# Stick-breaking attention taken from right to left, its scans cut in two pieces

## The chip, the cores and the metric

The kernel runs on one core of one Trainium2 chip. The metric is the device time of one execution in microseconds (us). TensorE is called PE, VectorE DVE, ScalarE ACT and GpSimd POOL, as in the profile.

## The reference

Two layers of a decoder trunk on 1024 tokens of width 1024: RMSNorm, two token mixers side by side (a dilated sliding-window attention and a stick-breaking attention) behind gates, a residual, then a gated ConvFFN and a residual. The change touches only the stick-breaking attention, four heads of 64 in each layer:

```python
def block(args):                       # 128 queries of block i, all heads
    z = jnp.einsum('bhqc,bhkc->bhqk', q_blk, kt) * scale
    causal = key_pos[None, :] < qpos[:, None]
    log_stay = jnp.where(causal, jax.nn.log_sigmoid(-z), 0.0)
    later = lax.cumsum(log_stay, axis=3, reverse=True) - log_stay
    attn = jnp.where(causal, jnp.exp(jax.nn.log_sigmoid(z) + later), 0.0)
    return jnp.einsum('bhqk,bhkc->bhqc', attn, vt)
```

Each weight is sigmoid(z) of its own key times the product of (1 - sigmoid(z)) over all later keys up to the query. The kernel forms that product of the later keys directly, as a running product from the right end of a row to its left end.

## The kernel before

Nearly all matmuls run in fp32 pieces: an operand is split into a high and a low part (ACT casts, DVE subtracts; `split`, lines 129 and 130), and products are sums of several matmuls.

PE's instructions are issued in the order in which the program writes them. In the mixers the order on DVE, ACT and POOL is chosen when the kernel is built, by priorities and a cost model; `tc.high_priority` moves an instruction ahead.

The stick-breaking work of a layer is 16 **items**, made by `stick_item(pr, s, qp)`: four heads (pr, s), and for each head qp = 0 to 3. An item covers two query blocks of 128 (its rows a = 0 and 1; block i = 2qp + a), and row a has L = 128 (i + 1) keys. An item has two score steps and qp + 1 pairs of a turn and an apply:

- `score(a)` (lines 610 to 628) computes the scores of one row in chunks of up to 512 keys from left to right into a PSUM bank (tag `s`, two banks; PE, lines 584 and 585). DVE adds the mask to the last 128 columns (line 623). ACT writes `beta` = sigmoid(z) (line 624) and `stay` = sigmoid(-z) (line 625). DVE then scans the whole row of `stay` from right to left (line 627) and multiplies `beta` by it, shifted by one (line 628).
- `turn(kb)` transposes the 128 x 128 blocks of the key blocks kb and kb + 1, of both rows, on PE (line 638) and splits them (`sbh`, `sbl`). `apply(kb)` multiplies them with the values (line 649) into one PSUM bank over all kb. The turns go from kb = 0 to kb = 2qp; the last one holds the diagonal blocks, and after its apply `fold` adds the two halves.

Both rows' `beta` tiles have the tag `p4` (four buffers, two for each item). `stay` holds both rows of an item and has the tag `e8` (six buffers, shared with the keys, queries and the output of this attention).

`attend` runs the items one after the other and weaves in the score steps of the next: with the sequence turn, late apply of the item before, turn, apply, ... of an item of qp + 1 turns, the first score step of the next item stands ahead of the first entry and the second one some way into the sequence. Behind every entry `dense.advance(rate)` issues pieces of other projections (`k_ps`, `q_ps`, `v_ps`, `r_ps`), 0.68 of a step for each entry in this stage, so that PE has work between the parts of an item. The neighbouring attention stages and the FFN are not touched.

Of the kernel before, what the change touches and what calls it, by code (L numbers as in the profile page):

```python
# [6 lines left out]
F32 = mybir.dt.float32  # L7
# [3 lines left out]
AF = mybir.ActivationFunctionType  # L11
ALU = mybir.AluOpType
# [3 lines left out]
P = 128  # L16
T = 1024
# [27 lines left out]
AHEAD = 200  # L45
# [7 lines left out]
def trunk_kernel(ctx, tc, x, norm1, w_in, b_gate, w_br, w_o, norm2, w_up, conv_w, conv_b, w_down, norm_f, out, depth=None, probe=None):  # L53
    nc = tc.nc
    act, dve, pe, pool = nc.scalar, nc.vector, nc.tensor, nc.gpsimd
# [4 lines left out]
    sb = ctx.enter_context(tc.tile_pool(name="sb", bufs=1))  # L60
# [10 lines left out]
    zero = cp.tile([P, 1], F32, name="zero")  # L71
    pool.memset(zero, 0.0)
    mask_b = cp.tile([P, P], BF16, name="mask_b")
# [42 lines left out]
    def bank(tag, name):  # L116
        return ps.tile([P, 512], F32, tag=tag, name=name)
# [4 lines left out]
    def big(name, dtype=F32):  # L122
        return sb.tile([P, 2, T], dtype, tag="e8", bufs=6, name=name)
# [459 lines left out]
    def scores(o, qt, ql, k):  # L583
        pe.matmul(o, qt, k, start=True, stop=False, skip_group_check=True)
        pe.matmul(o, ql, k, start=False, stop=True, skip_group_check=True)

    def parts(src, n, name):

        hi, lo = small(name + "h", F32R), small(name + "l", F32R)
        with tc.high_priority(offset=AHEAD):  # L590
            split(hi[:, :n], lo[:, :n], src[:, :n])
        return hi, lo

    def fold(dst, o):

        n = o.shape[-1]
        tmp = small("fold")
        with tc.high_priority(offset=AHEAD):
            act.copy(tmp[0:64, :n], o[64:128, :])
            dve.tensor_tensor(dst, o[0:64, :], tmp[0:64, :n], ALU.add)  # L600


    def stick_item(pr, s, qp):
        if "ob" not in R:
            R["ob"] = big("ob")
        q, k, vt, ob = R["qb", pr], R["kb", pr], R["vb"], R["ob"]
        hd = 2 * pr + s
        rows, st, shared = {}, {}, {}

        def score(a):  # L610
            i = 2 * qp + a
            L = P * (i + 1)
            bt = rows[a] = sb.tile([P, T], F32, tag="p4", bufs=4, name="beta")
            if a == 0:
                st[0] = big("stay")
            sv = st[0][:, a, :]
            for c0 in range(0, L, 512):
                w = min(512, L - c0)
                z = bank("s", "z")
                scores(z[:, :w], *(t[:, s, i * P : i * P + P] for t in q), k[:, s, c0 : c0 + w])  # L620
                with tc.high_priority(offset=AHEAD):
                    if c0 + w == L:
                        dve.tensor_tensor(z[:, w - P : w], z[:, w - P : w], mask_b, ALU.add)
                    act.activation(bt[:, c0 : c0 + w], z[:, :w], AF.Sigmoid)
                    act.activation(sv[:, c0 : c0 + w], z[:, :w], AF.Sigmoid, scale=-1.0)  # L625
            rev = sv[:, 0:L][:, ::-1]
            dve.tensor_tensor_scan(rev, rev, zero[:, 0:1].to_broadcast([P, L]), 1.0, ALU.mult, ALU.add)  # L627
            dve.tensor_tensor(bt[:, 0 : L - 1], bt[:, 0 : L - 1], sv[:, 1:L], ALU.mult)

        def blocks(kb):  # L630

            return [(j, a) for j in range(2) for a in range(2) if kb + j <= 2 * qp + a]

        def turn(kb):
            tp = bank("t", "sb_t")
            todo = blocks(kb)
            for c, (j, a) in enumerate(todo):
                pe.transpose(tp[:, c * P : c * P + P], rows[a][:, (kb + j) * P : (kb + j + 1) * P], ident)
            shared[kb] = parts(tp, len(todo) * P, "sb")

        def apply(kb):
            last = kb == 2 * qp
            if kb == 0:
                shared["o"] = bank("o", "sb_o")[:, :256]
            o = shared["o"]
            for j in range(2):
                c = P if last and j else 0
                for p in (0, 1):
                    pe.matmul(
                        o[:, c:256],  # L650
                        vt[(kb + j) // 4][:, (kb + j) % 4, hd, :],
                        shared[kb][p][:, 256 * j : 256 * j + 256 - c],
                        start=(kb == 0 and j == 0 and p == 0),
                        stop=(last and j == 1 and p == 1),
                        skip_group_check=True,
                    )
            if last:
                fold(ob[64 * s : 64 * s + 64, pr, qp * 256 : (qp + 1) * 256], o)
                if (pr, s, qp) == (1, 1, 3):
                    nc.sync.dma_start(obd, ob)  # L660

        sc = [lambda: score(0), lambda: score(1)]
        return sc, [(lambda kb=kb: turn(kb), lambda kb=kb: apply(kb)) for kb in range(0, 2 * qp + 2, 2)]


    def near_item(pr, s):
# [479 lines left out]
    def mixer(l, pending):  # L1146
# [37 lines left out]
        for pr in range(2):  # L1184
            for i in range(8):
                needs = ["b1"] if pr else []
                items.append((f"B{pr}{i}", needs, [], RATE[0], lambda pr=pr, i=i: stick_item(pr, i // 4, i % 4)))
# [687 lines left out]
```

## Time and profile before

| what | value |
|---|---|
| median of 3 runs | 2715.49 us (2715.37 to 2717.81) |
| the profiled execution | 2714.47 us, its span 2712.6 us |
| mean granted clock of PE | 0.997 |
| busy share of PE / DVE / ACT / POOL | 98% / 78% / 49% / 27% |
| stick-breaking items, layer 1 | about 69 to 231 us of the span |
| stick-breaking items, layer 2 | about 1410 to 1576 us of the span |

A row of the timeline gives start, duration, engine, line, operation, output and inputs, partitions x elements, and in square brackets the idle time of the engine ahead of it with what ended that. PEld is PE's weight load. A row of the waits gives who waited for whom, the sum in us, how many times, and the longest. Matmuls are pipelined, so a matmul of 512 columns shows 0.39 us but the next one can start 0.23 us after it.

### The profile page before, as it was taken

What the parts mean: (1) busy time and instruction counts of PE and PEld (TensorE: products, weight loads), DVE (VectorE), ACT (ScalarE), POOL (GpSimd) and SP (SyncE); (2) the same over time, 40 slices, a digit from 0 to 9 for tenths busy, and PEclk for the clock granted to TensorE, in tenths of its full rate; (3) what the DMA queues carried; (4) which work ended last, traced back from release to release, by engine and by line L of the source; (5) the groups of instructions that cost most, each with busy time, mean ns of one, the idle gap of its engine ahead of it and who ended that gap; (6) DMA issues with size and microseconds to landing.
All of it is one profiled execution on the core that took longest, in us unless ns stands there. A gap on an engine that the chain in (4) does not pass through costs nothing. (4 is left out here: it accounts for less than half of the span.)

```text
span 2712.6 us, 37003 instructions
## 1 busy us (share of the span) xinstructions
PE 2657.8 (98%) x13098; PEld 2227.5 (82%) x13098; DVE 2105.9 (78%) x3104; ACT 1330.4 (49%) x2458; POOL 742.1 (27%) x537
## 2 busy tenths in 40 slices
PE   8999999999999999999999989999999999999999
PEld 8877788888888888888888778888788888888888
DVE  6877876675789988897658888766858888998865
ACT  5656534464455555432335665434545545554225
POOL 2004133322233434321220041332212433443210
PEclk9999999999999999999999999999999999999999
DMA  4023389863235444688401234997722444446863
GB/s 153 20 80 123 123 229 246 207 226 121 85 117 171 141 154 147 223 320 320 154 32 36 84 111 136 250 230 211 248 85 79 148 152 143 171 141 253 333 246 122
DMA packets 397637, 445.72 MB, mean 164 GB/s; under 512 B 21660, under 2 KB 318988, under 8 KB 395916
## 3 DMA queue, kind: packets, MB, share of 16 engines
q1 hardware_dynamic: 397452, 443.35, 51.4%
q8 instruction: 104, 1.70, 0.3%
q14 instruction: 81, 0.66, 0.1%
HBM read 300.61 MB, written 142.67 MB: 163 GB/s over the span
## 5 line engine op out<-in xcount | busy, mean ns | idle before, releaser
L130 DVE TENSOR_TENSOR w_lo<-up_a,w_hi 128x512 fp32r<-128x512 f32 x240 | 237.2, 995 | 20.5 <-ACT w_hi L129 20.5
L129 ACT CAST w_hi<-up_a 128x512 fp32r<-128x512 f32 x240 | 149.5, 623 | 184.1 <-PE u_a L890 45.6
L1631 DVE TENSOR_TENSOR x<-x,d_ps 128x512 f32<-128x512 f32 (+1 forms) x228 | 152.2, 672 | 76.9 <-PE d_ps L1625 76.0
L1362 POOL TENSOR_TENSOR cv<-cv 128x512 f32<-128x512 f32 x88 | 132.1, 1513 | 248.8 <-DVE cv L1357 138.9
L130 DVE TENSOR_TENSOR w_lo<-w_raw,w_hi 128x512 fp32r<-128x512 f32 x176 | 132.5, 756 | 67.8 <-ACT w_hi L129 67.3
L129 ACT CAST w_hi<-w_raw 128x512 fp32r<-128x512 f32 x176 | 109.2, 621 | 125.9 <-PE o_ps L156 68.6
L129 ACT CAST w_hi<-in_a 128x512 fp32r<-128x512 f32 x140 | 86.8, 620 | 147.6 <-PE i_a L890 83.2
L130 DVE TENSOR_TENSOR g<-cv,g 128x512 fp32r<-128x512 f32 x154 | 152.4, 991 | 5.2 <-ACT g L129 2.7
L1623 PE MATMUL d_ps<-gd_in,w_hi 128*128 128x512 f32 (+1 forms) x340 | 130.2, 383 | 1.3 <-ACT w_hi L129 1.1
L1625 PE MATMUL d_ps<-gd_in,w_lo 128*128 128x512 f32 (+1 forms) x340 | 129.8, 382 | 0.0
L1624 PE MATMUL d_ps<-gd_in,w_hi 128*128 128x512 f32 (+1 forms) x340 | 129.7, 382 | 0.0
L889 PE MATMUL u_a<-hh,w_hi 128*128 128x512 f32 x320 | 124.7, 390 | 0.5 <-DVE u L1513 0.5
L889 PE MATMUL u_a<-t_hi,w_hi 128*128 128x512 f32 x320 | 124.6, 389 | 0.0
L891 PE MATMUL u_a<-t_hi,w_lo 128*128 128x512 f32 x320 | 124.5, 389 | 0.0
L890 PE MATMUL u_a<-hl,w_hi 128*128 128x512 f32 x320 | 124.5, 389 | 0.0
L891 PE MATMUL u_a<-hh,w_lo 128*128 128x512 f32 x320 | 124.5, 389 | 0.0
L890 PE MATMUL u_a<-t_lo,w_hi 128*128 128x512 f32 x320 | 124.5, 389 | 0.0
L130 DVE TENSOR_TENSOR w_lo<-in_a,w_hi 128x512 fp32r<-128x512 f32 x140 | 116.0, 828 | 4.1 <-ACT w_hi L129 3.7
L1018 POOL TENSOR_TENSOR in_a<-in_a 128x512 f32<-128x512 f32 x28 | 38.0, 1357 | 278.9 <-DVE w_lo L130 278.9
L627 DVE TENSOR_TENSOR_SCAN stay<-stay,zero 128x128 f32<-128x128 f32 (+3 forms) x64 | 89.0, 1390 | 32.2 <-ACT stay L625 31.6
L1623 PE MATMUL d_ps<-gd_in,wd 128*128 128x512 f32 (+1 forms) x292 | 113.9, 390 | 0.0
L129 ACT CAST g<-cv 128x512 fp32r<-128x512 f32 x154 | 95.0, 617 | 38.2 <-POOL cv L1362 29.7
(390 smaller groups left out, 8747.7 us busy)
## 6 DMA issues: line engine op xcount, KB each, us to landing
gd<-g SPq DMA_DIRECT2D x154, 512.0 KB, 3.7
gd_in<-gd SPq DMA_DIRECT2D x154, 512.0 KB, 6.4
up_a<-in_w_up_dram SPq DMA_DIRECT2D x80, 512.0 KB, 5.8
in_a<-in_w_in_dram SPq DMA_DIRECT2D x56, 512.0 KB, 6.2
w_raw<-in_w_in_dram SPq DMA_DIRECT2D x104, 256.0 KB, 3.0
t_kq<-tk SPq DMA_DIRECT2D x64, 384.0 KB, 7.8
wd_raw<-in_w_down_dram SPq DMA_DIRECT2D x22, 1024.0 KB, 13.0
gin<-gs SPq DMA_DIRECT2D x32, 512.0 KB, 4.4
```

What stands on the lines that cost most here:

```text
L129: act.copy(hi, src)
L130: dve.tensor_tensor(lo, src, f32(hi), ALU.subtract)
L627: dve.tensor_tensor_scan(rev, rev, zero[:, 0:1].to_broadcast([P, L]), 1.0, ALU.mult, ALU.add)
L889: pe.matmul(o, w[0][:, c], rh, start=(first and i == 0), stop=False, skip_group_check=True)
L890: pe.matmul(o, w[0][:, c], rl, start=False, stop=False, skip_group_check=True)
L891: pe.matmul(o, w[1][:, c], rh, start=False, stop=(last and i == 3), skip_group_check=True)
L1018: pool.tensor_tensor(a11, a22, a11, ALU.subtract)
L1362: return lambda: pool.tensor_tensor(dst, a, b, ALU.subtract)
L1623: pe.matmul(o[:, sub], wh[:, c], gh[:, sub], start=(i == 0 and k in (0, 4, 5)), stop=False, skip_group_check=True)
L1624: pe.matmul(o[:, sub], wh[:, c], gl[:, sub], start=False, stop=False, skip_group_check=True)
L1625: pe.matmul(o[:, sub], wl[:, c], gh[:, sub], start=False, stop=(i == m - 1), skip_group_check=True)
L1631: dve.tensor_tensor(x, x, o[:, sub], ALU.add)
```

## The change

Items with qp of 2 and 3 (five to eight key blocks in a row) are scored from right to left. The first score step now does the right parts (keys from 512 on) of both rows, the second one the left parts (keys 0 to 511) of both rows; the scan of a left part starts from the last value of the right one, and each part has a product of its own. Items with qp of 0 and 1, whose rows have at most 512 keys, keep one step for each row. In all items ACT writes `stay` ahead of `beta`, both `beta` tiles are taken at the first step, and turns and applies go from the diagonal (kb = 2qp) down to kb = 0.

```diff
-        def score(a):
+        def begin():
+            for a in range(2):
+                rows[a] = sb.tile([P, T], F32, tag="p4", bufs=4, name="beta")
+            st[0] = big("stay")
+
+        def score(a, c0):
             i = 2 * qp + a
             L = P * (i + 1)
-            bt = rows[a] = sb.tile([P, T], F32, tag="p4", bufs=4, name="beta")
-            if a == 0:
-                st[0] = big("stay")
-            sv = st[0][:, a, :]
-            for c0 in range(0, L, 512):
-                w = min(512, L - c0)
-                z = bank("s", "z")
-                scores(z[:, :w], *(t[:, s, i * P : i * P + P] for t in q), k[:, s, c0 : c0 + w])
-                with tc.high_priority(offset=AHEAD):
-                    if c0 + w == L:
-                        dve.tensor_tensor(z[:, w - P : w], z[:, w - P : w], mask_b, ALU.add)
-                    act.activation(bt[:, c0 : c0 + w], z[:, :w], AF.Sigmoid)
-                    act.activation(sv[:, c0 : c0 + w], z[:, :w], AF.Sigmoid, scale=-1.0)
-            rev = sv[:, 0:L][:, ::-1]
-            dve.tensor_tensor_scan(rev, rev, zero[:, 0:1].to_broadcast([P, L]), 1.0, ALU.mult, ALU.add)
-            dve.tensor_tensor(bt[:, 0 : L - 1], bt[:, 0 : L - 1], sv[:, 1:L], ALU.mult)
+            bt, sv, w = rows[a], st[0][:, a, :], min(512, L - c0)
+            z = bank("s", "z")
+            scores(z[:, :w], *(t[:, s, i * P : i * P + P] for t in q), k[:, s, c0 : c0 + w])
+            with tc.high_priority(offset=AHEAD):
+                if c0 + w == L:
+                    dve.tensor_tensor(z[:, w - P : w], z[:, w - P : w], mask_b, ALU.add)
+                act.activation(sv[:, c0 : c0 + w], z[:, :w], AF.Sigmoid, scale=-1.0)
+                act.activation(bt[:, c0 : c0 + w], z[:, :w], AF.Sigmoid)
+            rev = sv[:, c0 : c0 + w][:, ::-1]
+            right = 1.0 if c0 + w == L else sv[:, c0 + w : c0 + w + 1]
+            dve.tensor_tensor_scan(rev, rev, zero[:, 0:1].to_broadcast([P, w]), right, ALU.mult, ALU.add)
+            e = min(c0 + w, L - 1)
+            dve.tensor_tensor(bt[:, c0:e], bt[:, c0:e], sv[:, c0 + 1 : e + 1], ALU.mult)
...
         def apply(kb):
-            last = kb == 2 * qp
-            if kb == 0:
+            first = kb == 2 * qp
+            if first:
                 shared["o"] = bank("o", "sb_o")[:, :256]
...
-            if last:
+            if kb == 0:
                 fold(ob[64 * s : 64 * s + 64, pr, qp * 256 : (qp + 1) * 256], o)
...
-        sc = [lambda: score(0), lambda: score(1)]
-        return sc, [(lambda kb=kb: turn(kb), lambda kb=kb: apply(kb)) for kb in range(0, 2 * qp + 2, 2)]
+        def part(a):
+            if a == 0:
+                begin()
+            if qp < 2:
+                score(a, 0)
+            else:
+                for b in range(2):
+                    score(b, 0 if a else 512)
+
+        return [lambda: part(0), lambda: part(1)], [(lambda kb=kb: turn(kb), lambda kb=kb: apply(kb)) for kb in range(2 * qp, -2, -2)]
```

More of the change, by code (lines that the diff above doesn't have):

```diff
@@ L646, in apply @@
             for j in range(2):
-                c = P if last and j else 0
+                c = P if first and j else 0
                 for p in (0, 1):
@@ L652, in apply @@
                         shared[kb][p][:, 256 * j : 256 * j + 256 - c],
-                        start=(kb == 0 and j == 0 and p == 0),
-                        stop=(last and j == 1 and p == 1),
+                        start=(first and j == 0 and p == 0),
+                        stop=(kb == 0 and j == 1 and p == 1),
                         skip_group_check=True,
                     )
-            if last:
+            if kb == 0:
                 fold(ob[64 * s : 64 * s + 64, pr, qp * 256 : (qp + 1) * 256], o)
```

## The prediction

> **What bounds the kernel now.** I read the page first, then the stretches of the two layers in which the stick-breaking items run (69 to 231 us and 1410 to 1576 us), then the waits of TensorE in them.
>
> ```profile
> PE 2657.8 (98%) x13098; PEld 2227.5 (82%) x13098; DVE 2105.9 (78%) x3104; ACT 1330.4 (49%) x2458; POOL 742.1 (27%) x537
> 69.00:231.00 162.00, 153.20 (x900) 131.45 (x899) 132.97 (x202) 100.05 (x211) 3.79 (x4) 0.99 0.21 62
> 1410.00:1576.00 166.00, 155.42 (x902) 133.08 (x901) 135.38 (x201) 98.81 (x210) 9.12 (x9) 0.98 0.20 60
> ```
>
> TensorE (PE) is busy 98% of the span, so time is to be had only where PE stands still. The stretch rows give length, then busy time of PE, weight loads, VectorE (DVE), ScalarE (ACT) and GpSimd, then the granted clock: PE idles 8.8 + 10.6 = 19.4 us in the two stretches, DVE works 82% of them, and the DMA share is 0.2. The waits of PE there, layer by layer (us, times, longest):
>
> ```profile
> PE sb_t L638 <- DVE beta L628: 7.5, 6, 2.2
> PE sb_t L638 <- DVE beta L628: 9.2, 8, 2.2
> PEld z L584 <- ACT stay L625: 2.0, 4, 0.9
> PEld z L584 <- ACT stay L625: 1.9, 3, 0.9
> ```
>
> So 16.7 of the 19.4 us are transposes (L638) that wait for the product of L628. Which items are they? An item is one head and two query blocks; I call items 0 to 3 by qp. Four waits belong to items 0 and 1:
>
> ```profile
> 78.93 0.55 PE L638 MATMUL sb_t<-ident,beta 128*128 128x128 f32 x3 [0.94 <-DVE beta L628]
> 1414.26 0.33 PE L638 MATMUL sb_t<-ident,beta 128*128 128x128 f32 x1 [0.24 <-DVE beta L628]
> 1416.48 0.66 PE L638 MATMUL sb_t<-ident,beta 128*128 128x128 f32 x2 [1.89 <-DVE beta L628]
> 1423.36 0.55 PE L638 MATMUL sb_t<-ident,beta 128*128 128x128 f32 x3 [0.51 <-DVE beta L628]
> ```
>
> They make 3.6 us. The other ten, 13.1 us, are first turns of items 2 and 3 of the later heads: each time the first of four transposes (query row 0) runs and the second (row 1) stands. The longest, with its chain:
>
> ```profile
> 175.47 0.40 PE L584 MATMUL z<-kt,qt 128*128 128x512 f32 x1
> 175.93 0.40 PE L584 MATMUL z<-kt,qt 128*128 128x512 f32 x1
> 179.10 0.30 DVE L623 TENSOR_TENSOR z<-z,mask_b 128x128 f32<-128x128 f32 x1
> 180.56 2.29 DVE L627 TENSOR_TENSOR_SCAN stay<-stay,zero 128x1024 f32<-128x1024 f32 x1 [1.15 <-ACT stay L625]
> 183.21 1.22 DVE L628 TENSOR_TENSOR beta<-beta,stay 128x1023 f32<-128x1023 f32 x1
> 182.01 0.30 PE L638 MATMUL sb_t<-ident,beta 128*128 128x128 f32 x1
> 184.48 0.90 PE L638 MATMUL sb_t<-ident,beta 128*128 128x128 f32 x3 [2.17 <-DVE beta L628]
> ```
>
> Row 1's scores are done at 176.4 (a pair of 512 takes 0.46, 175.47 to 175.93), DVE gets to the mask at 179.1, the whole row must be scanned (2.29) and multiplied (1.22), and only then may its leftmost block be transposed, 2.4 us after PE came for it.
>
> **First turns from the right part.** After the change the first turn of items 2 and 3 takes blocks 2qp and 2qp+1, which lie in columns 512 and up. For both rows these are scored, scanned and multiplied in the first step. That step is issued where row 0 is now: for item 3, before the whole seq of item 2's turns, some 13 us before the first turn (row 0's scores now start at 168.56, quoted below; first turn 182.01). The waits of these ten go. The idle figure understates each: from 182.01 to 184.48 are 2.47 us where 0.06 would do, so 2.41 lost for 2.17 shown, 0.24 more. Ten times: 13.1 + 2.4 = 15.5 us. The bounds are 13.1 (idle alone) and 17 (add the two first-head items 3, which show only in the weight loads, 0.5 us each, and a little more of the overlap). I take 15.5 + 0.5 = 16.0.
>
> **The clock after the long waits.** Six matmuls before and after the wait at 184.48:
>
> ```profile
> 180.45 0.40 PE L155 MATMUL r_ps<-hh,w_hi 128*128 128x512 f32 x1
> 181.84 0.22 PE L584 MATMUL z<-kt,qt 128*128 128x128 f32 x1
> 185.04 0.78 PE L155 MATMUL r_ps<-hh,w_hi 128*128 128x512 f32 x1
> 187.72 0.28 PE L649 MATMUL sb_o<-sbh,vb 128*128 128x256 f32 x1
> 184.00:186.00 2.00, 1.52 (x5) 1.37 (x6) 1.99 (x5) 0.73 (x3) 0.00 (x0) 0.56 0.00 0
> 1528.00:1532.00 4.00, 3.11 (x10) 2.54 (x11) 3.94 (x7) 1.24 (x5) 0.00 (x0) 0.64 0.22 65
> 230.00:234.00 4.00, 4.00 (x24) 3.49 (x25) 2.97 (x9) 3.00 (x5) 0.00 (x0) 1.00 0.59 172
> ```
>
> Six take 1.39 us from 180.45 and 2.68 us from 185.04; the granted clock there is 0.56. That is 1.2 us lost behind the wait (less 0.1 that any turn costs), and the twin in layer 2 (0.64 over four us) as much: 2.4 us come back with the waits. Behind item 3 of the last head (230 to 234 us) the clock stays at 1.00, so I count two only. The Trainium skill, "TensorE: Matmul & The Clock Gate", section "What's actually happening", has the clock halved after at least one idle window of about 3.4 us; this trace disagrees, since it fell behind an idle of 2.17 us. By that rule these waits would be too short to cost any clock, nothing would come back here, and the sum below would be smaller by these 2.4 us.
>
> **ACT writes stay ahead of beta.** A scan needs only stay. In item 1 (one chunk of 512, nothing else changed) DVE stands at the scan until ACT has done both sigmoids:
>
> ```profile
> 160.08 1.23 DVE L627 TENSOR_TENSOR_SCAN stay<-stay,zero 128x512 f32<-128x512 f32 x1 [0.70 <-ACT stay L625]
> 162.08 0.31 PEld L638 LDWEIGHTS sb_t<-ident,beta 128*128 128x128 f32 x3 [0.36 <-DVE beta L628]
> 1551.37 0.31 PEld L638 LDWEIGHTS sb_t<-ident,beta 128*128 128x128 f32 x3 [0.42 <-DVE beta L628]
> ```
>
> A sigmoid of 512 is about 0.5 us of ACT, less than the 0.70 of idle, so scan and product come 0.5 us sooner. The small waits of item 1, four of this kind (first and last shown), go: 1.2 us of their 1.5. The four waits of the first heads quoted above hang on a loaded DVE; I leave them.
>
> **What it costs.** DVE gets a second scan and a second product for each row of items 2 and 3: 2 items, 4 heads, 2 layers, 2 rows, 32 of each.
>
> ```profile
> L627 DVE TENSOR_TENSOR_SCAN stay<-stay,zero 128x1024 f32<-128x1024 f32 x8 | 18.3, 2292 | 9.2 <-ACT stay L625 9.2
> L627 DVE TENSOR_TENSOR_SCAN stay<-stay,zero 128x512 f32<-128x512 f32 x8 | 9.8, 1225 | 5.5 <-ACT stay L625 5.4
> L628 DVE TENSOR_TENSOR beta<-beta,stay 128x1023 f32<-128x1023 f32 x8 | 9.7, 1216 | 0.1
> L628 DVE TENSOR_TENSOR beta<-beta,stay 128x511 f32<-128x511 f32 x8 | 5.5, 682 | 0.1
> ```
>
> 2 x 1.225 - 2.292 = 0.16 and 2 x 0.682 - 1.216 = 0.15 us, so 32 x 0.31 = 9.9 us of DVE, against some 60 us in which DVE idles in the two stretches: no charge on PE. No row shows a scan whose start value is a column; I bound it by 0 and by one more fixed part (0.16 x 32 = 5 us of DVE, also covered) and take 0; a gain I exclude, as nothing is left out. Matmuls, sigmoids, masks and transposes keep their number and widths; no DMA is moved, SP and POOL get nothing, and the store of ob stays behind the last apply.
>
> The scores of item 2's first step become 128 and 256 wide, where they were 512 and 128. The second of them waits today for the bank that item 1's last sigmoid frees (the z rows above). That bank comes free at the same time, but PE arrives earlier: a 512 pair takes 0.46 us, a 128 pair 0.17 (181.84 to 182.01). Six items 2 wait already: 6 x 0.29 = 1.7 us, at most 8 x 0.29 = 2.3.
>
> The second turn of an item now needs the left part, two scans and two products of 512. In item 2 it is close:
>
> ```profile
> 164.31 0.39 PE L584 MATMUL z<-kt,qt 128*128 128x512 f32 x1
> 168.56 0.39 PE L584 MATMUL z<-kt,qt 128*128 128x512 f32 x1
> 170.40 0.95 DVE L628 TENSOR_TENSOR beta<-beta,stay 128x767 f32<-128x767 f32 x1
> 173.64 0.60 PE L638 MATMUL sb_t<-ident,beta 128*128 128x128 f32 x4
> ```
>
> Today DVE ends the item at 171.35. With the same work in another order and 4 x 0.15 more it ends at about 172.0; the second turn, its 0.6 us of wait ahead gone, comes at 173.0. So 1 us in hand, which not every item will have; I take 0.2 us for each of 8, 1.6 us (between 0 and 3). In item 3 the second turn needs only the right part and the left one has several us.
>
> **Sum:** -16.0 - 2.4 - 1.2 + 1.7 + 1.6 = -16.3 us. The profiled execution took 2714.47 us (span 2712.6), the median is 2715.49: 2698.2 by the first, 2699.2 by the second, which I give. Bounds of the same case: -13.1 - 1.0 + 2.3 + 3 = -8.8 (no clock back) gives 2707; -17 for the waits, -2.9 for the clock (twice 0.36 of 4 us), -1.5 for item 1 and -1.9 for the first-head wait at 1416.48, with no new cost, is -23.3 and gives 2692.
>
> **Rivals.** *The wait moves to the second turn* of items 2 and, by less, 3. For it: DVE takes 2.7 us to reach a mask (176.4 to 179.1), and a margin of 1 us is less. Against: in the same stretch its total work grows by 0.6 us only. If 2.5 us get in front, each of 8 waits 1.5 us: 12 of the 16 are given back, about 2711.
>
> *Slower: the one stay buffer holds ACT, and ACT holds the score banks.*
>
> ```profile
> 216.38 0.60 ACT L625 ACTIVATE stay<-z 128x512 f32<-128x512 f32 x1 [1.40 <-DVE beta L628]
> ```
>
> The new item's first write of stay stands until the old item's last product. With stay ahead of beta this wait is at the head of the step; behind it on ACT queue the other three sigmoids, and the casts of the turns. Four sigmoids of item 3's right parts take some 1.8 us, then both z banks come free for the second step, whose scores PE issues 6 us after the first step's. It decides once left products end after 173.1 (174.9, that is 175.47 less the 0.6 us saved, minus 1.8), 1.1 us later than I put them. At 3 us late, 8 items 3 wait 1.9 us for a bank and 8 items 2 wait 2 us at the second turn: 31 us added, 16 saved, about 2730. Against: today's stall of 1.4 us does not reach PE.
>
> *The change doesn't do what it says:* if order is kept by whole tiles, the first turn waits for the left products as well, the waits stay and grow by the 0.3 to 0.6 us that DVE has more in each of 16 items, some 7 us: about 2722. Against it, these:
>
> ```profile
> 68.91 0.68 DVE L537 SCALAR_TENSOR_TENSOR ql<-q_ps,qt 64x512 fp32r<-64x512 f32 x1 [1.07 <-ACT qt L536]
> 69.50 0.28 PE L585 MATMUL z<-kt,ql 128*128 128x128 f32 x1
> 69.61 0.69 DVE L538 SCALAR_TENSOR_TENSOR ql<-q_ps,qt 64x512 fp32r<-64x512 f32 x1
> ```
>
> The matmul at 69.50 reads other columns of ql while two writes that stand before it in the program are still unfinished: order is kept by region.
>
> **How the numbers follow.** Forecast 0.75, wait at the second turn 0.10, held banks 0.10, whole tiles 0.05. About 0.2% (5.4 us) can be told from no change. Below 2710.1 lies the forecast: faster 0.75. Between falls most of the second case and a little of the others: same 0.11. Slower 0.14. The range runs from the forecast's best, 2692, to 2713, which takes in the second case.
>
> **What would show it.** Right: the group PE sb_t waiting for beta falls from 16.7 to about 4 us, no granted clock below 0.9 behind item 3 of the third heads, scans x96 with sum near 94 us, z waits near 6 us. Wrong: a new wait of the second turn on L628's product, waits of z on stay's sigmoid above 10 us, or first turns that still wait for a 512-wide left product.

## The result and the profile after

The kernel after takes 2702.5 us (median of 4 runs, 2699.0 to 2704.0); the kernel before, run beside it, 2716.4 us (4 runs, 2715.4 to 2717.8). The ratio is 0.995, with a 95% interval of 0.9938 to 0.9963. The forecast was 2699.2 us in a range of 2692 to 2713. The profiled execution after took 2702.83 us (span 2700.9), 11.6 us less than the one of before.

Two stretches of the timeline that hold the stick-breaking items of layers 1 and 2 up to the last item's first turns (length, then busy time and count on PE, weight loads, DVE, ACT and POOL, granted clock, DMA share, GB/s):

```profile
69.00:225.00 156.00, 150.61 (x904) 131.62 (x903) 136.42 (x234) 98.16 (x211) 3.80 (x4) 1.00 0.21 63
1403.00:1563.00 160.00, 152.03 (x909) 132.51 (x908) 138.74 (x233) 97.45 (x210) 9.81 (x9) 1.00 0.21 62
```

PE idles 5.4 + 8.0 = 13.4 us where it idled 19.4, and DVE's share grows from 82% to 87%: 6.8 us more work in shorter stretches. The stretches used so far, before and after, stop 12 to 14 us before the last turn of a layer, which starts at 243.7 and 1588.5 us before (not at 231 and 1576, as the table of the profile before has it) and at 236.6 and 1576.9 after. From the first score product to the end of that turn PE idles 21.1 us before and 15.9 after. The waits of PE in the same two stretches (who waited for whom, us in sum, times, longest):

```profile
PE r_ps L155 <- DVE ql L538: 1.9, 1, 1.9
PE z L584 <- ACT beta L625: 1.4, 3, 0.6
PE sb_t L640 <- DVE beta L630: 1.3, 1, 1.3
PE sb_o L651 <- DVE sbl L130: 0.7, 2, 0.4
...
PE sb_t L640 <- DVE beta L630: 3.2, 2, 1.9
PE z L584 <- ACT beta L625: 2.1, 3, 1.2
PE r_ps L155 <- DVE ql L538: 1.9, 1, 1.9
PE sb_o L651 <- DVE sbl L130: 0.8, 2, 0.4
```

Over the whole run the transposes wait 4.5 us for the beta product instead of 16.6, and all three waits that are left are of first heads: the ten of items 2 and 3 are gone. In their place stands a wait that the page of before does not have: a product `r_ps` of the gate projection waits for the second half of an eviction of queries (line 538). The place that answers to the chain shown of before, item 3 of the third head in layer 1, on DVE and PE:

```profile
173.34 0.69 DVE L630 TENSOR_TENSOR beta<-beta,stay 128x511 f32<-128x511 f32 x1
...
177.50 2.46 DVE L628 TENSOR_TENSOR_SCAN stay<-stay,zero 128x512 f32<-128x512 f32 x2
179.87 1.27 DVE L630 TENSOR_TENSOR beta<-beta,stay 128x512 f32<-128x512 f32 x2
...
183.72 0.69 DVE L538 SCALAR_TENSOR_TENSOR ql<-q_ps,qt 64x512 fp32r<-64x512 f32 x1
```

```profile
180.25 0.51 PE L640 MATMUL sb_t<-ident,beta 128*128 128x128 f32 x3
184.57 0.47 PE L155 MATMUL r_ps<-hh,w_hi 128*128 128x512 f32 x1 [1.95 <-DVE ql L538]
```

The right parts of both rows are multiplied by 174.0, six us before the first turn comes for them at 180.25. The left ones end at 181.1, less than a us after that turn, while row 1's product before ended at 184.4. So even the left parts are some 3 us earlier, although DVE has more to do. PE then stands until 184.4 for a query eviction that DVE reaches last. Before, the same eviction ended two us later, and no wait for it shows there; PE was late itself (the third head's first turn and the slow clock behind it):

```profile
185.83 0.70 DVE L538 SCALAR_TENSOR_TENSOR ql<-q_ps,qt 64x512 fp32r<-64x512 f32 x1
```

Two more long waits of after, out of PE's timeline, and then the granted clock (the figure behind the POOL count) in four stretches: the two places where it had fallen before, 184 and 1528 us, and behind these two waits:

```profile
1409.35 0.44 PE L640 MATMUL sb_t<-ident,beta 128*128 128x128 f32 x2 [1.94 <-DVE beta L630]
1568.74 0.39 PE L584 MATMUL z<-kt,qt 128*128 128x256 f32 x1 [1.96 <-DVE st L702]
```

```profile
184.00:188.00 4.00, 3.43 (x18) 2.96 (x19) 3.01 (x8) 1.74 (x5) 0.00 (x0) 1.00 0.58 187
1410.00:1414.00 4.00, 2.75 (x15) 2.21 (x14) 3.78 (x8) 2.91 (x7) 0.00 (x0) 1.00 0.03 8
1528.00:1532.00 4.00, 4.00 (x25) 3.42 (x24) 2.08 (x3) 2.01 (x4) 0.00 (x0) 1.00 0.85 245
1568.00:1572.00 4.00, 3.26 (x10) 2.75 (x11) 3.08 (x11) 3.15 (x9) 0.00 (x0) 0.63 0.40 128
```

In this execution it stays at 1.00 until 1568 us, while the last item's turns still run, and falls there. How much of that is the kernel and how much chance, two more stretches show, the first of before, behind the wait of 1.89 us at 1416.48 that the prediction quotes without its clock, the second of the kernel after, profiled again:

```profile
1416.00:1420.00 4.00, 3.52 (x10) 2.88 (x11) 3.00 (x7) 2.55 (x6) 0.00 (x0) 0.57 0.00 0
186.00:190.00 4.00, 4.00 (x14) 3.28 (x14) 1.59 (x5) 0.59 (x1) 0.00 (x0) 0.57 0.42 138
```

So before has a third fall, and in the second profile of the kernel after the clock falls behind the very wait that left it at 1.00 in the first (`r_ps` for `ql`, 1.95 us in both). Each fall in these traces lasts 3.4 us at half clock, or twice that, so one of 3.4 us costs PE at most 1.7 us. The scans and products of DVE, all shapes together (sum, mean ns; then the idle time of DVE ahead of them and what ended it), after and then before:

```profile
L628 DVE TENSOR_TENSOR_SCAN stay<-stay,zero 128x128 f32<-128x128 f32 (+2 forms) x96 | 93.2, 981 | 10.1 <-ACT stay L624 9.4
L630 DVE TENSOR_TENSOR beta<-beta,stay 128x127 f32<-128x127 f32 (+2 forms) x96 | 54.1, 570 | 6.2 <-ACT sbh L129 0.5
```

```profile
L627 DVE TENSOR_TENSOR_SCAN stay<-stay,zero 128x128 f32<-128x128 f32 (+3 forms) x64 | 89.0, 1390 | 32.2 <-ACT stay L625 31.6
L628 DVE TENSOR_TENSOR beta<-beta,stay 128x127 f32<-128x127 f32 (+3 forms) x64 | 49.0, 766 | 0.9
```

DVE works 9.3 us more in them, and stands 22 us less at a scan for its sigmoid. This second number is the one that I had not looked at, although two of the rows that the prediction quotes carry 9.2 and 5.4 us of it.

### The profile page after: what moved, and what is told of

Its sections match the earlier page's. It is cut to its first block, busy times and chain, and to the rows that moved or that the text cites. A ratio compares the mean times of both kernels' runs of the same rounds, so it can differ in the third digit from the quotient of the medians.

```text
span 2700.9 us, 37123 instructions
## 1 busy us (share of the span) xinstructions
PE 2651.9 (98%) x13098; PEld 2228.1 (82%) x13098; DVE 2106.5 (78%) x3168; ACT 1327.4 (49%) x2458; POOL 746.4 (28%) x537
## 5 line engine op out<-in xcount | busy, mean ns | idle before, releaser
L1633 PE MATMUL d_ps<-gd_in,wd 128*128 128x512 f32 (+1 forms) x292 | 113.9, 390 | 0.0
L418 POOL TENSOR_TENSOR nrm<-nrm,sq 128x512 f32<-128x512 f32 x29 | 40.6, 1399 | 264.2 <-ACT sq L416 263.5
L1635 PE MATMUL d_ps<-gd_in,wd 128*128 128x512 f32 (+1 forms) x292 | 112.8, 386 | 0.0
```

The costliest lines, as they stand in the source:

```text
L418: (adds or (dve if e % 3 == 1 else pool)).tensor_tensor(acc, acc, sq, ALU.add)
L1633: pe.matmul(o[:, sub], wh[:, c], gh[:, sub], start=(i == 0 and k in (0, 4, 5)), stop=False, skip_group_check=True)
L1635: pe.matmul(o[:, sub], wl[:, c], gh[:, sub], start=False, stop=(i == m - 1), skip_group_check=True)
```

## The experiments

I compare two things: the time against the kernel before on the same chip, and the length of the stages, from the first score product of a layer's items to their last turn, both layers summed. That length comes from one profiled execution. The kernel after, profiled twice, gave 167.3 + 173.3 = 340.5 and 169.6 + 171.2 = 340.8 us: a single layer can differ by 2.3 us between executions, so I read nothing into sums that lie within 2 or 3 us of each other. The column on the half clock is what PE lost by it in these stages at most (the time at half clock, halved). All 20 falls of the 14 profiled executions (the 13 of the table and the first of after) stand behind waits of PE of 1.80 to 2.84 us; 19 other waits of that size left the clock at 1.00, one of 2.65 us among them. Which waits of this size cost clock is chance as far as these runs show, so two stage lengths are best compared with this column taken off.

| kernel | median us | ratio to before, 95% interval | stages us | of it by half clock, us | DVE idle at the scan for `stay`: us, times | turns waiting for beta: us, times |
|---|---|---|---|---|---|---|
| before | 2717.9, 2717.4, 2717.4 | 1 | 352.5 | 5.1 | 31.6, 39 | 16.6, 14 |
| turns_only | 2716.1 | 0.9996 (0.9987 to 1.0004) | 350.4 | 3.4 | 29.7, 39 | 16.0, 16 |
| act_order | 2706.8 | 0.9957 (0.9946 to 0.9969) | 344.4 | 1.7 | 19.3, 36 | 9.0, 9 |
| order_and_turns | 2705.6 | 0.9959 (0.9947 to 0.997) | 342.5 | 0 | 19.3, 36 | 8.8, 9 |
| pieces_only | 2707.5 | 0.9963 (0.995 to 0.9975) | 342.4 | 1.7 | 16.4, 21 | 9.8, 14 |
| beta_first | 2705.2 | 0.9956 (0.9943 to 0.9969) | 344.8 | 5.1 | 16.5, 21 | 5.2, 8 |
| left_first | 2706.7 | 0.9955 (0.9942 to 0.9968) | 341.9 | 1.7 | 9.3, 18 | 6.4, 9 |
| row_by_row | 2712.9 | 0.9989 (0.9979 to 0.9998) | 347.4 | 5.1 | 12.7, 24 | 2.8, 2 |
| queries_ahead | 2711.2 | 0.998 (0.9971 to 0.9989) | 342.8 | 5.1 | 11.5, 22 | 3.2, 2 |
| after_again | 2703.2 | 0.9947 (0.9935 to 0.996) | 340.8 | 1.7 | 9.4, 18 | 4.5, 3 |
| mask_pe | 2696.7 | 0.9923 (0.991 to 0.9935) | 333.6 | 0 | 15.5, 13 | 2.6, 3 |
| start_more | 2715.3 | 0.999 (0.9981 to 0.9999) | 354.2 | 5.1 | 13.6, 26 | 2.8, 2 |
| dve_load | 2716.6 | 0.9997 (0.9988 to 1.0006) | 340.1 | 0 | 9.4, 18 | 4.5, 3 |

The three values of before belong to the three sets of kernels that ran together: act_order, beta_first, left_first and turns_only; pieces_only, order_and_turns, row_by_row and queries_ahead; and the last four rows. turns_only, act_order and order_and_turns are edits of the kernel before, all others of the kernel after.

**The parts of the change: turns alone, ACT's order alone, and each undone**

turns_only is the kernel before with its turns and applies from the diagonal block on, scans and steps as they were:

```diff
...
-        return sc, [(lambda kb=kb: turn(kb), lambda kb=kb: apply(kb)) for kb in range(0, 2 * qp + 2, 2)]
+        return sc, [(lambda kb=kb: turn(kb), lambda kb=kb: apply(kb)) for kb in range(2 * qp, -2, -2)]
```

> The kernel before with turns and applies from the diagonal on, all else as before: whole rows scanned at once, a step for each row. Theory: nothing moves, since every block of row 1 waits for the whole scan; within 2 us of 2716, first-turn waits near 16 us, though now in items 2 at the first turn's second or third transpose. Rival (the order of the turns is enough): 10 us or more faster.

The interval holds 1: no change. The waits of the turns in turns_only:

```profile
PE sb_t L638 <- DVE beta L628: 16.0, 16, 2.0
```

The waits are those of before. Since the scan and the product of a row are whole here, the first turn waits for the whole row whichever block it takes. This run shows only that the order of the turns is worth nothing by itself. Undoing that order in the changed kernel (left_first) asks more:

```diff
-            first = kb == 2 * qp
-            if first:
+            last = kb == 2 * qp
+            if kb == 0:
...
-        return ... for kb in range(2 * qp, -2, -2)]
+        return ... for kb in range(0, 2 * qp + 2, 2)]
```

> The changed kernel with its turns and applies from left to right again; scores, scans and products stay from right to left in pieces. Theory: the first turn of items 2 and 3 needs the left products of both rows, the last thing that DVE makes for the item, so all first-turn waits are back and some longer: 0 to 8 us slower than the kernel before, 2716 to 2724. Rival (shorter scans, or order on ACT, make the gain): still 8 us or more faster.

Here the first turn needs the left parts again, as before the change, and nearly all of the gain stays: the rival of the text is right, its theory wrong. The waits of first turns of items 2 and 3 in left_first are six; the first, out of the timeline of PE:

```profile
170.68 0.55 PE L640 MATMUL sb_t<-ident,beta 128*128 128x128 f32 x3 [0.45 <-DVE beta L630]
```

All six (0.45, 0.30, 0.21, 0.51, 0.25, 0.21) make 1.9 us, where the ten of before made 13.1. So it is not that the first turn was freed from the left part: the left part itself comes in time.

act_order is the kernel before with ACT's two sigmoids exchanged, and nothing else:

```diff
-                    act.activation(bt[:, c0 : c0 + w], z[:, :w], AF.Sigmoid)
                     act.activation(sv[:, c0 : c0 + w], z[:, :w], AF.Sigmoid, scale=-1.0)
+                    act.activation(bt[:, c0 : c0 + w], z[:, :w], AF.Sigmoid)
```

> The kernel before with one edit: ACT writes stay ahead of beta. Theory (the first turns of items 2 and 3 are freed because they need right parts only): each of the ten first-turn waits gets shorter by the 0.4 to 0.5 us that DVE idled at a scan for ACT, the small waits of item 1 go, the waits of 2.17 us may stop costing clock: 5 to 8 us faster, about 2709, and first turns still wait (8 to 11 us in the group). Rival (order on ACT is the whole gain): 13 to 14 us faster, first-turn waits gone.

One exchanged line takes 11 us off the median and 8 us off the stages (4.7 without the half clock), where I had priced it at 1.2. What it does on DVE and to the turns, by the waits of both engines in act_order:

```profile
DVE stay L627 <- ACT stay L624: 19.3, 36, 0.8
```

```profile
PE sb_t L638 <- DVE beta L628: 9.0, 9, 1.9
```

DVE's idle time at the scan falls by 12 us and the turns' waits by 7.6, over rows of nearly every length (at scans of 1024 from 9.2 to 5.3 us) and not in item 1 alone. beta_first is the reverse, the changed kernel with the two lines in their old order:

> The changed kernel with beta written ahead of stay again. Theory: first turns of items 2 and 3 stay free of waits, the small waits of item 1 come back (1.2 us) and the left products end 0.5 us later: 11 to 13 us faster than the kernel before, about 2704. Rival (order on ACT is the whole gain): the time of the kernel before, 2716.

Its stages are 344.8 us, some 4 us longer than those of after, of which 3.4 are half clock, and its time (0.9956) is not told from that of after (0.995). So one part alone gives most of the gain, and the changed kernel without that part loses little: the parts stand in for each other. This led to another theory. DVE takes its work in the order that was chosen when the kernel was built. When it stands at a scan, everything behind it (products, splits, query evictions) stands too. Less standing moves the whole queue forward, and any edit that does this gets nearly the same time back from PE's waits.

**Whole scans or pieces**

pieces_only is the changed kernel with left_first's turns and beta_first's order, so that of the change only the steps and the pieces are left. order_and_turns is the kernel before with act_order's line and turns_only's range, so that all but the pieces is done.

> Pieces from right to left in two steps, but beta ahead of stay and turns from left to right: of the three parts of the change the first alone. The length of a stage below is from its first score matmul to the start of its last turn in the trace (kernel before: 164.5 and 168.2 us, the changed kernel 157.7 and 160.8). New theory (what matters is when the last product of an item is done on DVE against PE's arrival; ACT order and pieces each bring it forward, the order of turns hardly counts): stages together 5 to 9 us shorter than before, time 2707 to 2711. First theory (the first turn has to be freed from the left part): first-turn waits of 16 us stay and nothing is gained, 2716 or slower.

> Stay ahead of beta and turns from the diagonal on, but whole rows scanned at once, a step for each row. New theory: as with the ACT order alone (stages together 9.8 us shorter), within 1.5 us of that; about 2707. First theory: without right parts the order of turns gives nothing, so the same number; against both, if the turns alone need only part of the rows' ends: 12 us or more.

Both came out near the new theory's numbers, 2707.5 and 2705.6 us, and far from the first theory's 2716. (Where these texts speak of the start of the last turn, the marks used were those of the second turn of the last head's item 3; the stages in the table go to the last turn of all.) The two kernels have no edit in common and come out alike, 0.9963 and 0.9959, stages 342.4 and 342.5 us. The sum of the two would be twice that, 20 us of stage; all together give 12, little more than either. (Without the half clock: 6.7 and 4.9 us for the two, and 8.6 for all together, so they replace each other in part.)

row_by_row keeps the pieces, ACT's order and the turns, but each step does one row again, its right part and then its left:

```diff
-                for b in range(2):
-                    score(b, 0 if a else 512)
+                for c0 in (512, 0):
+                    score(a, c0)
```

> The changed kernel with a row in each step (its right part, then its left part) in place of right parts of both rows and then left parts. First theory: the first turn of item 3 now needs the right part of row 1 from the second step, and mask, scan of 512 and product end about when PE comes: up to 0.5 us of wait for some of 8 items, 2 to 4 us slower than the changed kernel. New theory: the last product is no later than in the kernel with ACT order alone and the first turn needs half of it: within 2 us of the changed kernel; both masks' wait on DVE in the second step decides.

It loses most of the gain, and both theories missed that: it is 10 us slower than the kernel after, where the new one allowed 2 and the first one 2 to 4. It is also the run that speaks most plainly against my first account: the turns wait only 2.8 us in it, less than in after, and yet it is only 0.0011 faster than before. A row of its timeline, and the stretch behind that row:

```profile
186.22 0.47 PE L155 MATMUL r_ps<-hh,w_hi 128*128 128x512 f32 x1 [2.27 <-DVE ql L538]
```

```profile
188.00:192.00 4.00, 4.00 (x17) 3.44 (x16) 2.01 (x4) 1.86 (x4) 0.00 (x0) 0.61 0.24 70
```

DVE ends the eviction of queries at 186.1 where after had it at 184.4, PE waits there instead, and the clock falls behind it. Taking away the first turns' waits is worth little if the queue behind them is not earlier too. Without the half clock its stages are 342.3 us, as those of act_order (342.7) and order_and_turns (342.5), which have no pieces, and 3.5 above those of after (338.8). So what the pieces add to the order on ACT comes from having row 1's right part in the first step. The other 3.4 us of its stages are half clock in this one profile; of its twelve runs eight took 2710 to 2713 us and four 2718 to 2719.

**Moving the late eviction, and filling the first heads**

Two tries at the waits that are left in after. queries_ahead gives the eviction of the queries priority:

```diff
+        with tc.high_priority(offset=AHEAD):
             for q2, src in ((qa, o[0:64]), (qb, o[64:128])):
...
             dve.scalar_tensor_tensor(lb[64:128], o[64:128], scale, f32(qb[64:128]), ALU.mult, ALU.subtract)
```

> The changed kernel with the two instructions of DVE and four of ACT that empty the query bank (lines 534 to 538) put ahead in priority, as the masks and sigmoids are. Theory: the waits of r_ps for ql in the third heads (3.8 us in two) go, and nothing else of that size is behind them: stages 3 to 4 us shorter than in the changed kernel, about 2699. Rival: the instructions moved ahead push scans back, the wait turns up as first-turn or bank waits, and the time is that of the changed kernel, 2702.

Neither half of the text has it: the kernel takes 2711.2 us, 9 more than the rival's number and than after. The wait for the eviction is 3.1 us where it was 3.8, so the edit hardly does what it was meant for. Its stages are 2 us longer, within what two executions differ by. The rest was lost outside the stages, 4.8 us between them and 3.4 behind the second: between them PE waits for splits of the neighbouring attention (`p0l`) 6.0 us instead of 3.7, and the rest I can't place. Why a priority in one stage changes the order in another I did not follow up.

start_more puts two more steps of the neighbouring projections ahead of the first turn of the stage's first item, where PE comes too early (once in each layer, not for each head as the text says):

```diff
                 for f in sc:
                     f()
                     dense.advance(rate)
+                dense.step()
+                dense.step()
```

> The changed kernel, with two more steps of the neighbouring products ahead of the first turn of the first item of each head, where 1.29, 1.94 and 1.30 us of waits for the beta product are left. Theory (PE comes to that first turn too early since nothing else fills the time): these three waits go, 2 to 4 us shorter, 2699 to 2701 us. Rival (the filling is then missing further on, at the wait for the queries' second eviction and at the scores): within 1 us of the changed kernel, the wait moved.

It is 12 us slower than after_again, and neither theory nor rival was right in size. In the waits of PE of start_more the turns' wait is smaller, 2.8 us, and two others are large:

```profile
PE z L586 <- ACT beta L627: 8.3, 4, 2.8
PE r_ps L155 <- ACT q1s L995: 7.8, 4, 2.5
```

The steps are a fixed stock. Used earlier, they are missing later, which fits the new waits: score products for a bank, the gate's products for ACT's `q1s`. The rival has the waits of the scores, not the one for the queries' eviction, which is gone, and the price is 12 us, not 1.

**DVE's load by itself**

after_again is the kernel after beside the last three runs, their base:

> The changed kernel itself, as the base of the three beside it on the same chip. Both theories: 2702 to 2704 us, stages of the stick-breaking items 340.5 us in sum (167.3 and 173.3), idle time of DVE at its scan for the sigmoid 9 to 10 us.

mask_pe adds the mask of the diagonal block on PE where DVE added it:

```diff
...
+            if c0 + w == L:
+                pe.matmul(z[:, w - P : w], ident_b, mask_b, start=False, stop=True, skip_group_check=True)
             with tc.high_priority(offset=AHEAD):
-                if c0 + w == L:
-                    dve.tensor_tensor(z[:, w - P : w], z[:, w - P : w], mask_b, ALU.add)
```

> The changed kernel, with the mask of the diagonal block added on TensorE (a product of the identity and the mask into the scores' bank) where VectorE added it: VectorE loses 64 additions of some 0.29 us (18.5 us) and a hop between scores and sigmoid, TensorE gains 64 products of 128 columns (some 4 to 8 us). Theory that VectorE's queue, by the time at which it ends its work, sets what is left of PE's waits in the stages (13.4 us of PE idle): the wait for the queries' second eviction (3.8 us) goes, VectorE's idle time at the scan for the sigmoid falls or stays, PE idle in the stages falls by 4 to 8 us, and the time stays within 3 us of the changed kernel, as much gained as the products cost. Rival (VectorE has slack, PE's work alone sets the time): PE idle is as before, and the time is 4 to 8 us longer than the changed kernel.

It takes 2696.7 us (5 runs, 2695.9 to 2698.8) against 2703.2 of after_again (5 runs, 2699.9 to 2706.4): 6.5 us less than the kernel after, and the best of all. The two stages as stretches, from the first score product to the end of the last turn, of mask_pe and then of after_again, and the waits of PE in the stages of mask_pe, layer 1 and then the two longest of layer 2:

```profile
69.60:235.50 165.90, 164.55 (x1002) 141.88 (x1001) 139.51 (x229) 108.88 (x234) 4.02 (x5) 1.00 0.24 73
1401.40:1570.40 169.00, 165.35 (x1002) 141.95 (x1002) 141.65 (x228) 108.37 (x234) 9.54 (x9) 1.00 0.23 70
70.20:240.30 170.10, 163.98 (x971) 142.79 (x970) 145.38 (x262) 107.16 (x236) 4.30 (x5) 0.99 0.24 71
1407.60:1579.50 171.90, 162.42 (x971) 141.46 (x970) 147.13 (x259) 106.11 (x233) 9.49 (x9) 1.00 0.23 70
```

```profile
PE r_ps L157 <- DVE ql L540: 0.6, 1, 0.6
PE sb_t L642 <- DVE beta L632: 0.3, 1, 0.3
PE z L586 <- ACT beta L627: 0.2, 1, 0.2
PE z L586 <- DVE st L704: 0.2, 1, 0.2
...
PE sb_t L642 <- DVE beta L632: 2.3, 2, 1.6
PE r_ps L157 <- DVE ql L540: 0.6, 1, 0.6
```

PE idles 5.0 us in the stages of mask_pe and 15.6 in those of after_again. The theory foresaw 4 to 8 us less idle and 10.6 came; it foresaw no more than 3 us of time, with the 64 products on PE priced at 4 to 8 us. They cost about 3.5: PE's busy time in the stages grows from 326.4 to 329.9 us, though after_again lost up to 1.7 us there by the half clock and mask_pe none. The stages are 7.2 us shorter. One part of my account falls here. DVE's idle time at the scan rises from 9.4 to 15.5 us while the kernel gets faster. Idle time there is a place to look, not a gauge; what counts is, by my reading, whether the work queued behind it is late for PE. row_by_row says the same the other way round: 19 us less of that idle time, and next to no gain.

dve_load was meant as the opposite, one more addition on DVE in each step:

```diff
...
+            dve.tensor_tensor(extra, extra, extra, ALU.add)
```

> The changed kernel, with one more VectorE addition (128x256, some 0.42 us) on a tile that nobody reads in each score step: 64 of them, some 27 us of VectorE. Theory (VectorE's queue sets the waits that are left in the stages): the first turns' wait and the wait for the queries' second eviction grow, stages 5 to 12 us longer in sum, 2708 to 2715 us. Rival (VectorE has slack there, 78% busy, and PE alone sets the time): within 2 us of the changed kernel.

It does not answer the question. The 64 additions (duration least, median and most in ns, then first and last start in us), and the first 69 us of the span as a stretch:

```profile
L669 DVE TENSOR_TENSOR extra<-extra x64: 404/424/1531, 1.3 to 67.7; 128x256 f32<-128x256 f32 x64
```

```profile
0.00:69.00 69.00, 53.02 (x327) 48.07 (x328) 62.16 (x125) 30.91 (x60) 17.50 (x27) 0.88 0.42 138
```

Since nothing ties them to a step, the order chosen at build time put all of them ahead of the first stage. There DVE works 62.2 us of the 69 and PE 53.0, PE gets to the first stage at 81.0 us, 11 later than in after_again, and that is most of the 13 us that are lost; the stages are as long as in after. Whether mask_pe gains by the load it takes from DVE or by the hop that it takes out between scores and sigmoid stays open: a load that is tied to the steps was not tried.

## Why the prediction was right, and where it was not

The time was right: 2699.2 forecast, 2702.5 measured, inside the range; 13.9 us less than before by the medians where 16.3 were worked out (11.6 by the two profiles, in which the stages are 11.9 shorter). The way there was right in half of its steps, so that the sum came out near is in part luck: one term was too large, one was much too small, a wait was left out, and the clock is chance.

**First turns from the right part, -16.0.** The size held: the ten waits are gone. The cause did not. I put them down to the first turn being freed from the left part; left_first, where it isn't, has 1.9 us of these waits left. And I took the waits removed as time gained. row_by_row shows that they are not the same: 13.8 us of turn waits gone, and 3 us of time by the ratio (4.5 by the medians). The first heads' waits, which I left as they were, grew by 0.9 us, so PE's rows give -12.1 for all turns. The 2.4 us that I added for what the idle figure understates were a little too much: transposes follow each other after 0.11 us (four of 0.27 take 0.60), not 0.06.

**The clock, -2.4.** At both places 0.56 and 0.64 became 1.00, but the term was luck. before has a third fall that I did not see (0.57 behind 1416.48), after has one of its own at 1568.74, and the second profile of after has one at 185.82. The waits of 1.8 us and more, each of which can cost clock, went from five to four (three in the second profile). The rule of the Trainium skill that the prediction names ("TensorE: Matmul & The Clock Gate", section "What's actually happening"), with an idle window of about 3.4 us, does not fit the other runs either: the clock fell behind 1.96 us in after, 1.94 us at 1412.94 in act_order and 2.27 us in row_by_row. Nor is there a length from which it always falls: 1.95 us at 184.57 in after, 1.99 us at 229.91 in before and 2.65 us at 1582.84 in dve_load left it at 1.00.

**ACT writes stay ahead of beta, -1.2.** The step that was mis-sized. I looked for the stall where PE's row showed it, in item 1, and left out that DVE stands at 39 scans for 31.6 us, which is one row of DVE's waits before. The edit alone is worth 8 us of stage (352.5 to 344.4), 4.7 without the half clock; undone in the changed kernel it costs some 4 (340.5 to 344.8), of which 0.9 are left without the half clock. In time it is 11 us alone, and undone not told from nothing. The sigmoid of 512 that I put at 0.5 us takes 0.60.

**DVE's extra work, covered.** The work was right: 93.2 us of scans where I said near 94, and 9.3 us more with the products where I said 9.9. That it costs PE nothing was not tested by itself: the same change takes 22 us of DVE's standing away.

**The z bank, +1.7 and the second turn, +1.6.** Scores waiting for ACT's sigmoid grew from 0.9 to 3.5 us in PE's rows, 2.6 us. Second turns never wait: 0. None of the three rivals came: no wait on a 512-wide left product, no held banks, no order by whole tiles.

**What was missing.** I asked what is late next only for the items' own parts. The next late thing was another piece of the same DVE queue, the queries' eviction, with 3.8 us. By PE's rows the account is -12.1 for the turns, +3.8 for the eviction, +2.6 for the scores and +0.7 for the applies, -5.0; PE's idle time in the whole stages fell by 5.2. The other 6.5 us are not in any wait: PE is busy 332.4 us in the stages before and 325.9 after, for the same matmuls. Of this the half clock is at most 3.4 (three falls before, one after), and so in part chance; the rest, 3 us, would be the slow starts behind waits, for which I had counted 2.4, but no run measures them by themselves. Outside the stages before and after differ by no more than 0.5 us; other runs differ there by several us, up and down, with no cause that I can show.

## What to carry to other kernels

On an engine whose order is fixed when the kernel is built, a stall belongs to all that is queued behind it: read how long and how often it stands for its first operand, exchange the two instructions that make that operand late before anything larger is rebuilt, and expect edits that move the same queue to replace each other in part, not to add up. A wait that goes is time gained only if what the waiting engine needs next is earlier as well, so follow the chain one step beyond. And work moved from the engine whose queue is late (DVE here, 78% busy) to the one that is 98% busy can pay, if it costs that one little: the mask on PE gave 6.5 us more for 3.5 us of products, by the load or by the hop. Last, before two profiles are compared, read the granted clock in both, since here one fall more or less is up to 1.7 us.

## What the runs showed of the hardware

The start of layer 2 has the longest of the first heads' waits that are left (1.94 us in after, 1.61 in mask_pe). DVE and POOL in after there:

```profile
1404.59 0.42 DVE L628 TENSOR_TENSOR_SCAN stay<-stay,zero 128x128 f32<-128x128 f32 x1
1405.12 1.13 DVE L630 TENSOR_TENSOR beta<-beta,stay 128x127 f32<-128x127 f32 x1
1406.18 1.78 DVE L628 TENSOR_TENSOR_SCAN stay<-stay,zero 128x256 f32<-128x256 f32 x1
1408.06 1.23 DVE L630 TENSOR_TENSOR beta<-beta,stay 128x255 f32<-128x255 f32 x1
```

```profile
1403.41 2.69 POOL L923 TENSOR_TENSOR h_sum<-h_sum,hh 128x512 f32<-128x512 f32 x2
1406.07 2.94 POOL L924 TENSOR_TENSOR h_sum<-h_sum,hh 128x512 f32<-128x512 f32 x2
```

While POOL adds (until 1409.0), a product of 127 columns takes 1.13 us, where the mean of its kind is 0.33, a scan of 256 takes 1.78 against 0.75, and a product of 255 takes 1.23 against 0.47. Each loses some 0.8 to 1.0 us, less than one addition of POOL (2.69 for two). The scan of 128 at 1404.59 takes its usual 0.42 all the same. The Trainium skill, "SBUF — State Buffer", section "Who interferes with whom", says that DVE and GpSimd share a pair of ports and that it is held as an exclusive lock; the durations agree with a wait for POOL's running instruction. dve_load, by its additions that nobody waits for, shows it better. DVE and then POOL in it:

```profile
49.86 1.34 DVE L669 TENSOR_TENSOR extra<-extra 128x256 f32<-128x256 f32 x3
53.46 2.97 DVE L669 TENSOR_TENSOR extra<-extra 128x256 f32<-128x256 f32 x2
56.95 3.73 DVE L669 TENSOR_TENSOR extra<-extra 128x256 f32<-128x256 f32 x3
```

```profile
51.24 3.46 POOL L925 TENSOR_TENSOR h_sum<-hl 128x512 f32<-128x512 f32 x2 [8.94 <-DMA tk<-none]
57.55 2.85 POOL L927 TENSOR_TENSOR h_sum<-h_sum,hh 128x512 f32<-128x512 f32 x2
```

The same addition takes 0.45 us ahead of POOL's work and 1.2 to 1.5 us while POOL adds `h_sum` (51.2 to 60.4 us). Under POOL's memsets, at 6.54 and 35.95 us, it takes 0.42 and 0.43. No run moved `h_sum` away from the start of layer 2, so that the first-head waits would go with it was not shown.
